# A planner in the source that orders all five engines, longest path first

## The chip, the cores and the metric

One core of one Trainium2 chip. The time is the device time of the whole program in microseconds; lower is better. The core has five engines, each of which works through a list of its own in order: TensorE (PE, with its weight loads PEld), VectorE (DVE), ScalarE (ACT), GpSimd (POOL) and SyncE (SP), which issues all the DMAs. Between engines, an instruction waits for semaphores.

## The reference

One step of a layer with two parallel mixers, for a prompt of 2048 rows and for 8 sequences of 8 new rows ("sample", with a cache of 2048 keys each), all float32:

```python
h = rmsnorm(x, norm_w)
z = h @ w_in                                  # 1024 -> 3600 columns
q, k, v, qb, kb, vb, g_lr, gate_a, gate_b = jnp.split(z, split_points(), axis=-1)
q = rope(rmsnorm(heads(q, H_A), q_norm_w), pos)
k = rope(rmsnorm(heads(k, H_A), k_norm_w), pos)
o_a = attend(q, k, v)                         # three dilated windows, mixed by their softmax sums
log_a = jax.nn.log_sigmoid(g_lr @ w_gate_up + b_gate) / GATE_TAU
o_b, s_fin = gla_chunked(qb, kb, vb, log_a, s0)   # gated linear attention, exact and causal
o_b = rmsnorm(o_b, gla_norm_w)
mixed = jnp.concatenate([o_a * silu(gate_a), o_b * silu(gate_b)], axis=-1)
y = x + mixed @ w_out
```

The three windows are (128, step 1), (512, step 4) and (2048, step 16), with 8 heads of 64. The outputs are y, the rotated keys, the values and the states.

## The kernel before

**Projections.** x is normed in 16 tiles of 128 rows, split into two float16 parts and turned; `project(name, tiles)` multiplies a tile with a block of w_in (v, q, k, qkb, g, vb, gb; 512 columns, g in two halves of 272 and 256) in 24 float16 matmuls into one of two accumulators in PSUM (tag `Y`, names `acc_...`). The results go through VectorE and ScalarE to scratch tensors in device memory (`q_d`, `kp_d`, `vp_d`, ...), and are read back, some by a transposing DMA.

**Attention of the prompt.** `attend` makes a unit of four steps: s (scores, L408), p (a VectorE instruction that masks and finds the maximum, L416, and a ScalarE exponential with its sum, L419), t (transposes on TensorE, L426), pt (the turned p in two float16 parts, by ScalarE and VectorE, or by ScalarE twice and POOL, in turn, L388 to L393) and O (weighted values, L441). Its core:

```python
for n, (q, k) in enumerate(prods):                       # qk, L408
    PE.matmul(s_ps[:, i * w : (i + 1) * w], q, k, ...)
...
DVE.tensor_tensor_reduce(s[:, sl], s_ps[:, sl], mask, neg, BIG, ALU.add, ALU.min, nmf(i))
ACT.activation(s[:, sl], s[:, sl], AF.Exp, bias=nmf(i), scale=-1.0, accum_out=denf(i))
...
PE.transpose(p_ps[:, i * P : (i + 1) * P], t["s"][:, i * P : (i + 1) * P], ident[:])   # tr, L426
split([pt[:, c, w_] for c in range(2)], p_ps[:, w_], t["s"][:, w_])
...
PE.matmul(o_, t["pt"][:, c, ...], vf(i, b), ...)         # pv, L441
```

There are 128 units for the first two windows (two heads each) and 32 for the third (`branch3`, four heads each); `pipeline()` writes them so that three are under way. The tags S, PT and O have two PSUM buffers each.

**The rest.** `sample_scores` multiplies cached keys with queries (POOL `pr`, L980; VectorE `sck`, L981). `gla_core` runs the gated linear attention in seven levels per 256 rows: differences D (POOL), E (ScalarE), ks and qbd (VectorE), sc (TensorE, L247). `prompt_out` gathers a tile's parts (`combine`), turns them (`turned`, tm, L1453) and multiplies by w_out (`finish`, L1488) into two accumulators Y_t_0 and Y_t_1 of 24 matmuls each, which VectorE adds to x (L1495). `sample_pair` does the sample's attention over the cache (OS, L1737); its result goes through the scratch tensor `oa_d` to the sample's own output tile.

**What sets the order.** The Python code is written as generators that `weave` takes steps from in set ratios. The result is the program order, which a scheduler of the framework, with a timeline of its own, turns into one list per engine. Two places bind it: the first tiles' preparation holds ScalarE to the written order, and the loading of the blocks q and k is held behind the last low part of the block before:

```python
with tc.manual_schedule(engines={mybir.EngineType.Activation}):
    prep_first(load_w("v"))
...
with tc.issue_after(last_low[0].ins):
    at_once(load_w("q"))
```

Of the kernel before, what the change touches and what calls it, by code (L numbers as in the profile page):

```python
# [7 lines left out]
F32 = mybir.dt.float32  # L8
F32R = mybir.dt.float32r
F16 = mybir.dt.float16  # L10
BF16 = mybir.dt.bfloat16
# [4 lines left out]
PSUM = bass.MemoryType.PSUM  # L16
DRAM = bass.MemoryType.DRAM

P = 128
# [27 lines left out]
    "vb": (2048, 512),  # L47
    "gb": (3088, 512),
}


@with_exitstack
def tile_hymba(ctx: ExitStack, tc: tile.TileContext, A: dict):
    nc = tc.nc
    PE, ACT, DVE, POOL, SP = nc.tensor, nc.scalar, nc.vector, nc.gpsimd, nc.sync
# [293 lines left out]
    with ExitStack() as c1:  # L349
# [19 lines left out]
        sp = c_att.enter_context(tc.tile_pool(name="sp", bufs=3))  # L369
# [106 lines left out]
        last_low = [None]  # L476
# [189 lines left out]
        def at_once(gen):  # L666
            for _ in gen:
                pass
# [77 lines left out]
        done = set()  # L746
# [271 lines left out]
            return pool.tile([P, 512], F32, name=f"wr_q_{k}", tag=tag)[:]  # L1018

        fetch_w("q", places=q_place)  # L1020
        with tc.manual_schedule(engines={mybir.EngineType.Activation}):
            prep_first(load_w("v"))
        fetch_w("k")

        gnw = const1("gnw", [P, P], A["gla_norm_w"].to_broadcast([P, P]))
# [9 lines left out]
        for nm_, src in (("q", A["q_norm_w"]), ("k", A["k_norm_w"])):  # L1035
            i = "qk".index(nm_)
            w = tabs[:, 0, i]
# [27 lines left out]
        work, side = deque(), deque()  # L1065
# [74 lines left out]
        def first(m):  # L1140
            tiles = list(range(4 * m, 4 * m + 4))
            if m == 0:
                for name in "vqk":
                    for t in (["s"] if name == "v" else []) + tiles:
                        yield from project(name, [t])
                        if name == "v":
                            if t == 0:
                                with tc.issue_after(last_low[0].ins):
                                    at_once(load_w("q"))
                            elif t == 2:  # L1150
                                with tc.issue_after(last_low[0].ins):
                                    at_once(load_w("k"))
                                for f in range(4, 8):
                                    fetch(f)
                        elif name == "k":
                            prep(t + 4)
                            fetch(t + 8)
                return
            for t in tiles:
                for name in "vqk":  # L1160
                    if (name, t) == ("q", 15):
                        at_once(load_w("qkb"))
                    yield from project(name, [t])
                    dot_next(t)
# [27 lines left out]
        order = {"qkb": [12, 13, 14, 15, *range(12)]}  # L1192
# [51 lines left out]
        st = {"wgu": wgu, "E": [], "ks": [], "qbd": []}  # L1244
        for i in range(2):
            for lst, nm_, shape in (
# [3 lines left out]
                t = gst.tile(shape, F32, name=f"{nm_}{i}")  # L1250
# [141 lines left out]
        left = weave(host, gla_all, fetch, until=[host, fetch])  # L1392
# [4 lines left out]
        left = weave(host, gla_all, fetch, until=[gla_all])  # L1397
# [3 lines left out]
        for h in range(4):  # L1401
            p, j = divmod(h, 2)
# [11 lines left out]
        place = lambda t: slice(0, 1) if t == "s" else slice(t + 1, t + 2)  # L1414
# [190 lines left out]
        for nh in range(2):  # L1605
            t = cb1.tile([P, NT + 1], F32, name=f"inv_o{nh}")
# [4 lines left out]
        out = [prompt_out(), 2 * NT * KT + 30]  # L1611
# [180 lines left out]

        weave(out, [sample_attention(), 4 * 16])


# [1 line left out]
_INS = [  # L1797
# [90 lines left out]
```

## Time and profile before

| | |
|---|---|
| median of 3 runs | 1424.39 us (1419.62 to 1426.09) |
| profiled execution, first to last instruction | 1424.9 us; of its own time nothing else is on record, and the span is 0.5 us from the median |
| busy | PE 1285.0, DVE 1018.0, ACT 843.7, POOL 621.9 us |
| mean granted clock of TensorE | 0.966 |
| DMA | 283.27 MB; q1 uses 67.1% of 16 engines' span |

"Busy" of an engine is the time in which at least one of its instructions runs; matmuls overlap each other, so a busy TensorE isn't one at its peak. A line such as `L408 PE MATMUL s<-kk,qq 128*128 128x256 f16 x432 | 93.8, 335 | 17.5 <-DVE o L416 12.4` reads: line 408, engine, operation, output and inputs, shape, how many; busy us in total, mean ns of one; idle us of the engine just before them, and who ended that idle time.

### The profile page before, as it was taken

The numbers are of one execution on the slowest core, as the hardware profiler recorded it, in microseconds if no ns is written. First come the engines' busy times: TensorE is split into PE (matmuls) and PEld (weight loads), VectorE is DVE, ScalarE is ACT, GpSimd is POOL, SyncE is SP. The second block draws the span as 40 slices with busy tenths as digits, with TensorE's granted clock in tenths as the row PEclk, the third lists the DMA queues.
The fourth block names the chain that finished last, engine by engine and source line by source line (L and its number), as shares of the span: only waits on it lengthen the run. The fifth ranks groups of instructions, "written<-read, shape, count | busy, mean of one in ns | idle before, by whom it ended". The sixth has DMA issues, their size and how long they took to land.

```text
span 1424.9 us, 26506 instructions
## 1 busy us (share of the span) xinstructions
PE 1285.0 (90%) x8942; PEld 743.6 (52%) x8942; DVE 1018.0 (71%) x2459; ACT 843.7 (59%) x2259; POOL 621.9 (44%) x564
## 2 busy tenths in 40 slices
PE   5989999889898898996889999889999989999997
PEld 2434555455455554664667666666555434444343
DVE  6797697789798967666775357898877797773222
ACT  6466787667377775875677665777876542221120
POOL 0144355566577455554421486556551264340000
PEclk9999999999999899997999999999999999999998
DMA  8469756678966797888976444242235759998661
GB/s 297 156 188 255 192 161 150 182 203 215 240 165 173 208 288 239 260 217 228 234 190 179 149 123 116 87 153 91 88 119 176 267 179 344 359 316 267 221 215 63
DMA packets 246874, 283.27 MB, mean 199 GB/s; under 512 B 117889, under 2 KB 148690, under 8 KB 246738
## 3 DMA queue, kind: packets, MB, share of 16 engines
q1 hardware_dynamic: 246738, 281.57, 67.1%
q8 instruction: 71, 1.16, 0.4%
q14 instruction: 65, 0.53, 0.1%
HBM read 183.19 MB, written 75.24 MB: 181 GB/s over the span
## 4 chain that ended last, share of the span: by engine, by line
PE 35%; DVE 25%; DMA 16%; ACT 11%; issue 7%; POOL 4%; SPq 2%; DVEq 0%; POOLq 0%; ACTq 0%
PE Y L1488 7%; PE acc_g L1120 3%; PE acc_vb L1120 3%; PE acc_k L1120 3%; DMA k<-in_cache_k_win 2%; POOL pr L980 2%; PE s L408 2%; PE OS L1737 2%; PE acc_qkb L1120 2%; ACT p L419 2%; DMA o_d<-o 2%; DMA oc<-o_d 2%; DVE p L416 2%; PE acc_v L1120 2%; DMA T_q<-qp_d 2%
## 5 line engine op out<-in xcount | busy, mean ns | idle before, releaser
L980 POOL TENSOR_TENSOR pr<-k,qb 128x512 f32<-128x512 f32 x128 | 171.8, 1342 | 184.9 <-DVE sck L981 113.9
L1120 PEld LDWEIGHTS <-hr 128*128 128x128 f16 x1824 | 177.7, 100 | 138.2 <-issue 17.6
L419 ACT ACTIVATE p<-p,o 128x256 f32<-128x256 f32 (+1 forms) x384 | 173.1, 453 | 86.0 <-DVE o L416 83.3
L1120 PEld LDWEIGHTS <-hl 128*128 128x128 f16 x1248 | 123.2, 100 | 146.6 <-issue 22.2
L1488 PE MATMUL Y<-w_o,mh 128*128 128x512 f16 x768 | 182.9, 385 | 8.3 <-ACT mh L1454 4.9
L416 DVE CUSTOM_DVE_ANT_0 p<-s,m3w,scl_s 128x256 f32<-128x256 f32 (+1 forms) x384 | 143.6, 419 | 39.0 <-DMA o_d<-o 20.3
L393 POOL TENSOR_TENSOR pt<-p,pt 128x512 f16<-128x512 f32 (+1 forms) x80 | 98.3, 1229 | 139.6 <-ACT pt L392 107.3
L441 PE MATMUL O<-v,pt 128*128 128x128 f16 x1200 | 116.1, 224 | 25.3 <-POOL pt L393 10.0
L426 PE MATMUL t<-ident,p 128*128 128x128 f32 x600 | 119.0, 289 | 14.5 <-ACT p L419 9.2
L1488 PEld LDWEIGHTS <-mh 128*128 128x128 f16 x768 | 72.5, 99 | 103.7 <-issue 25.2
L408 PE MATMUL s<-kk,qq 128*128 128x256 f16 (+1 forms) x512 | 105.7, 326 | 17.5 <-DVE o L416 12.4
L981 DVE TENSOR_REDUCE sck<-pr 128x8 f32<-128x512 f32 x128 | 87.0, 680 | 44.0 <-POOL pr L980 43.7
L441 PEld LDWEIGHTS <-pt 128*128 128x128 f16 x1200 | 86.6, 101 | 54.6 <-POOL pt L393 13.6
L1120 PE MATMUL acc_g<-w_g,hr 128*128 128x272 f16 (+1 forms) x768 | 103.3, 285 | 1.9 <-DVE so_g L677 1.0
L1120 PE MATMUL acc_v<-w_v,hl 128*128 128x512 f16 x384 | 99.5, 405 | 4.6 <-DMA hl<-ht 3.7
L426 PEld LDWEIGHTS t<-ident,p 128*128 128x128 f32 x600 | 73.5, 146 | 43.2 <-ACT p L419 26.4
L1120 PE MATMUL acc_q<-w_q,hl 128*128 128x512 f16 x384 | 92.0, 380 | 1.9 <-ACT zs_q L703 1.4
L1120 PE MATMUL acc_k<-w_k,hl 128*128 128x512 f16 x384 | 91.3, 382 | 2.5 <-ACT w_k L658 1.3
L1454 ACT ACTIVATE mh<-tm 128x1024 f16<-128x1024 f16 x32 | 31.7, 1019 | 104.1 <-PE tm L1453 97.7
L1120 PE MATMUL acc_gb<-w_gb,hr 128*128 128x512 f16 x384 | 90.0, 388 | 2.1 <-DVE so_gb L677 2.1
L1120 PE MATMUL acc_vb<-w_vb,hr 128*128 128x512 f16 x384 | 89.3, 379 | 1.6 <-DVE so_g L677 1.6
L212 ACT ACTIVATE E<-D_e 128x256 f32<-128x256 f32 (+1 forms) x168 | 67.7, 411 | 27.1 <-DVE ks L219 17.6
(533 smaller groups left out, 2628.1 us busy)
## 6 DMA issues: line engine op xcount, KB each, us to landing
k<-in_cache_k_win SPq DMA_DIRECT2D x104, 256.0 KB, 4.3
sv<-in_cache_v_win SPq DMA_DIRECT2D x104, 256.0 KB, 5.4
hr<-h_d SPq DMA_DIRECT2D x44, 512.0 KB, 4.1
qb<-q_d SPq DMA_DIRECT2D x64, 256.0 KB, 4.6
oc<-o_d SPq DMA_DIRECT2D x48, 264.0 KB, 5.8
o_d<-o SPq DMA_DIRECT2D x64, 132.0 KB, 3.9
x<-in_x_prompt SPq DMA_DIRECT2D x16, 512.0 KB, 5.8
h_d<-hl SPq DMA_DIRECT2D x16, 512.0 KB, 4.7
```

Of the source, the lines that this page charges most:

```text
L212: ACT.activation(E[rows, i, :n], D[rows, half], AF.Exp, scale=1.0 / 16.0)
L393: POOL.tensor_tensor(l, f, h, ALU.subtract)
L408: PE.matmul(s_ps[:, i * w : (i + 1) * w], q, k, start=(n == 0), stop=(n == len(prods) - 1),)
L416: DVE.tensor_tensor_reduce(s[:, sl], s_ps[:, sl], mask, neg, BIG, ALU.add, ALU.min, nmf(i))
L419: ACT.activation(s[:, sl], s[:, sl], AF.Exp, bias=nmf(i), scale=-1.0, accum_out=denf(i))
L426: PE.transpose(p_ps[:, i * P : (i + 1) * P], t["s"][:, i * P : (i + 1) * P], ident[:])
L441: PE.matmul(o_, t["pt"][:, c, (i * nb + b) * P : (i * nb + b + 1) * P], vf(i, b), start=(n == 0), stop=(n == 2 * nb - 1),)
L980: POOL.tensor_tensor(pr[:], kt, qt, ALU.mult)
L981: DVE.tensor_reduce(out, pr[:].rearrange("p (u k d) -> p u k d", u=2, k=4), AX.X, ALU.add)
L1120: PE.matmul(z, a_[:, k, :], w[:, p_, k, cols], start=(k == 0 and i == 0), stop=(k == KT - 1 and i == 2),)
L1454: ACT.activation(mhl[:, a], pt[:], AF.Copy)
L1488: PE.matmul(Y[:], a_[:, k, :], w_[:, part, k, :512], start=(i == 0), stop=(i == len(prods) - 1),)
```

## The change

At the end of the kernel's Python code a class `Plan` reads all the traced instructions, finds what each depends on, gives each a price, and makes a list schedule of its own. Then it chains the instructions of each engine in that order, so that the framework's scheduler has no choice left:

```diff
+class Plan:
+    ENGINES = ("PE", "DVE", "Activation", "Pool", "SP")
+    def __init__(self, tc, nc, cross=35.0, traffic=1.15, lanes=8, room=212832):
...
+        self.read()
+        self.depend()
+        self.price()
...
+                if kind == "InstCustomDveAnt":
+                    late = (211 if by_row else 150) + 1.04 * n
...
+    def rank(self):
...
+            far[n] = max(
+                own + max((far[x] for x in self.nxt[n]), default=0.0),
+                max((far[x] for x in self.then[n]), default=0.0),
+            )
...
+    def order(self, prio, bias=0.0):
...
+            if len(out["SP"]) >= self.lanes:
+                free["SP"] = max(free["SP"], done[out["SP"][-self.lanes]] + self.cross + 20)
...
+            _, n = heappop(line)
+            out[e].append(n)
...
+            if e == "SP":
+                free[e] = t + self.busy[n]
+                queue = max(queue, free[e]) + self.late[n]
+                done[n] = queue + self.lands[n]
...
+                if (n in self.slow) != mode:
+                    s, mode = max(s, max(column) + 93), not mode
...
+    def fix(self, out):
...
+        for e, order in out.items():
+            for a, b in zip(order, order[1:]):
+                self.tc.add_manual_dep(
+                    self.ins[b], self.ins[a].name, info, reason="planned order"
+                )
...
-        with tc.manual_schedule(engines={mybir.EngineType.Activation}):
-            prep_first(load_w("v"))
+        prep_first(load_w("v"))
...
-                                with tc.issue_after(last_low[0].ins):
-                                    at_once(load_w("q"))
+                                at_once(load_w("q"))
...
+    plan = Plan(tc, nc)
+    far = plan.rank()
+    plan.fix(plan.order([-f for f in far], 2000.0)[1])
```

`far[n]` is the length of the longest chain of prices from instruction n to the end of the program. Whenever an engine is free, it takes of its ready instructions the one with the largest `far`. Equal values are taken by turns of the heap, in program order. In the planner a float32 matmul that isn't a transpose (`slow`) costs 93 ns more when the kind changes, and is preferred or put back by 2000 ns so that kinds stay together; a DMA waits until the eighth before it has landed; VectorE and POOL hold each other up where both read two operands from SBUF. Buffers are taken in program order, and a buffer's next tile waits for all users of the last. The number and kind of instructions on every engine stay the same. The two bindings above go. Lines after the class stand 489 further down: L408 is L897, L426 is L915, L1120 is L1608, L1488 is L1974.

Three places of the order. The first is TensorE's list where a unit of the third window (residue 9, first half) passes from s to t; the numbers at the ends of names count tiles. Before, from its last s on:

```order
L408 MATMUL s_3_9_0_8912<-T3_k_9_8879,T3_q_9_8877 128x128
L441 LDWEIGHTS pt_3_7_1_8850
L441 MATMUL O3_7_1_8933<-v3_7_8659,pt_3_7_1_8850 128x128
...
L426 MATMUL t_3_8_0_8901<-ident_79,p_3_8_0_8803 128x128
L441 LDWEIGHTS pt_3_7_1_8850
```

Now:

```order
L897 MATMUL s_3_9_0_8909<-T3_k_9_8876,T3_q_9_8874 128x128
L897 LDWEIGHTS T3_q_9_8874
L897 MATMUL s_3_9_1_8957<-T3_k_9_8876,T3_q_9_8874 128x128
L1608 LDWEIGHTS hr_1_8636
L1608 MATMUL acc_vb_1_10287<-w_vb_8471,hr_1_8636 128x512
L1608 LDWEIGHTS hr_1_8636
L1608 MATMUL acc_g1_1_10254<-w_g_6888,hr_1_8636 128x256
...
L915 MATMUL t_3_9_0_9005<-ident_79,p_3_9_0_8910 128x128
```

The first t of the unit stood 122 rows behind its last s, with steps of units 7 and 8 between them; now it stands 15 rows behind, the two halves of the unit are taken by turns, and projection matmuls of two accumulators fill the place.

The second place is the end of TensorE's list, the last output tile (15). Before:

```order
L1488 MATMUL Y_15_0_16950<-w_o0_13844,mh_15_16842 128x512
L1488 LDWEIGHTS mh_15_16842
L1488 MATMUL Y_15_0_16950<-w_o0_13844,mh_15_16842 128x512
L1488 LDWEIGHTS mh_15_16842
L1488 MATMUL Y_15_1_16976<-w_o1_14251,mh_15_16842 128x512
```

Now:

```order
L1974 MATMUL Y_15_1_16973<-w_o1_14248,mh_15_16839 128x512
L1974 LDWEIGHTS mh_15_16839
L1974 MATMUL Y_15_0_16947<-w_o0_13841,mh_15_16839 128x512
L1974 LDWEIGHTS mh_15_16839
L1974 MATMUL Y_15_1_16973<-w_o1_14248,mh_15_16839 128x512
```

Before, all 24 matmuls of Y_15_0 stood ahead of those of Y_15_1; now the two accumulators take turns to the end, as they do in the other output tiles.

The third place is the end of SP's list: `soo` is the last pair's attention output of the sample, which goes to `oa_d` and comes back as `oa_s`; `xr` are the rows of x to which a tile's output is added. Before:

```order
L1499 DMA out_y_prompt<-xr_14_16804 128x1024
L1781 DMA oa_d_71<-soo_3_16635 64x64 x2
L1477 DMA xr_15_16948<-in_x_prompt 128x1024
L1558 DMA oa_s_16881<-oa_d_71 64x256 x2
L1499 DMA out_y_sample<-xr_s_16907 64x1024
L1499 DMA out_y_prompt<-xr_15_16948 128x1024
```

Now:

```order
L2267 DMA oa_d_71<-soo_3_16632 64x64 x2
L1985 DMA out_y_prompt<-xr_13_16689 128x1024
L2044 DMA oa_s_16878<-oa_d_71 64x256 x2
L1963 DMA xr_s_16904<-in_x_sample 64x1024
L1985 DMA out_y_prompt<-xr_14_16801 128x1024
L1963 DMA xr_15_16945<-in_x_prompt 128x1024
L1985 DMA out_y_sample<-xr_s_16904 64x1024
L1985 DMA out_y_prompt<-xr_15_16945 128x1024
```

The sample's output through `oa_d` stood behind the output of tile 14; now it stands ahead of that of tile 13. On TensorE the last OS matmuls have moved from tile 14 and the transposes of tile 15 to tile 13.

More of the change, by code (lines that the diff above doesn't have):

```diff
@@ L1147, in first @@
                             if t == 0:
-                                with tc.issue_after(last_low[0].ins):
-                                    at_once(load_w("q"))
+                                at_once(load_w("q"))
                             elif t == 2:
-                                with tc.issue_after(last_low[0].ins):
-                                    at_once(load_w("k"))
+                                at_once(load_w("k"))
                                 for f in range(4, 8):
```

423 lines of the change are left out of this document (added).

## The prediction

> **What bounds the kernel now.** I read the page first, then the clock, the busy times by stage, the groups by form, and single stretches of the timeline.
>
> ```profile
> span 1424.9 us, 26506 instructions
> ...
> PE 1285.0 (90%) x8942; PEld 743.6 (52%) x8942; DVE 1018.0 (71%) x2459; ACT 843.7 (59%) x2259; POOL 621.9 (44%) x564
> ...
> core 0: 1424.9 us, clock 0.966
> ...
> PE 35%; DVE 25%; DMA 16%; ACT 11%; issue 7%; POOL 4%; SPq 2%; DVEq 0%; POOLq 0%; ACTq 0%
> ```
>
> TensorE is the engine to keep fed: it is busy 1285.0 of 1424.9 us, so 139.9 us are plain idle. The granted clock of 0.966 costs up to 1424.9 x 0.034 = 48 us more. But only 35% of the chain that ended last is TensorE; VectorE, ScalarE, DMAs and issue hold most of the rest. That is the picture of an order that leaves TensorE waiting, here for one engine and there for another. The next view says where; its columns are the stage, its length, then busy us of PE, PEld, DVE, ACT and POOL with instruction counts, the clock, the DMA share and GB/s.
>
> ```profile
> 0.00:100.00 100.00, 77.49 (x385) 36.57 (x385) 76.82 (x177) 56.37 (x104) 19.44 (x29) 1.00 0.63 211
> 100.00:400.00 300.00, 274.74 (x1732) 157.17 (x1733) 244.27 (x572) 201.44 (x570) 158.91 (x122) 0.97 0.76 200
> 400.00:500.00 100.00, 87.02 (x592) 54.98 (x591) 89.59 (x205) 74.53 (x207) 62.90 (x48) 0.93 0.69 187
> 500.00:600.00 100.00, 92.93 (x633) 56.58 (x631) 67.86 (x181) 71.37 (x202) 57.47 (x46) 0.97 0.90 260
> 600.00:700.00 100.00, 81.94 (x608) 55.12 (x607) 69.63 (x216) 65.07 (x206) 47.95 (x39) 0.88 0.86 231
> 700.00:800.00 100.00, 95.11 (x841) 69.98 (x839) 62.72 (x259) 78.14 (x283) 22.92 (x22) 1.00 0.69 176
> 800.00:900.00 100.00, 98.34 (x743) 61.93 (x741) 59.99 (x122) 57.18 (x149) 69.38 (x82) 1.00 0.44 124
> 900.00:1000.00 100.00, 87.39 (x812) 62.91 (x813) 87.06 (x184) 79.21 (x211) 58.31 (x70) 0.97 0.37 118
> 1000.00:1100.00 100.00, 91.18 (x722) 54.53 (x719) 81.11 (x170) 74.28 (x184) 43.62 (x51) 0.98 0.41 130
> 1100.00:1200.00 100.00, 88.89 (x493) 42.80 (x491) 79.37 (x177) 45.68 (x89) 40.72 (x34) 0.95 0.74 251
> 1200.00:1400.00 200.00, 192.90 (x1333) 83.72 (x1326) 93.96 (x200) 40.08 (x61) 40.25 (x31) 0.99 0.79 268
> 1400.00:1425.00 25.00, 17.07 (x68) 7.29 (x68) 5.66 (x8) 0.38 (x1) 0.00 (x0) 0.82 0.13 43
> ```
>
> Length minus PE busy gives the idle: 22.5 us in the first stage (start-up), 68.3 in 100 to 800 (projections woven with attention), 23.1 in 800 to 1100 (gated linear attention), 26.1 in 1100 to 1425 (output projection woven with the sample attention). Stages of the same kind differ: 18.1 us are lost in 600:700 and 4.9 in 700:800; 12.6 in 900:1000 and 1.7 in 800:900. The clock is low exactly where the idle is: 0.88, 0.93, 0.95, 0.82. One wait of each kind:
>
> ```profile
> 657.57 0.47 PE L426 MATMUL t<-ident,p 128*128 128x128 f32 x1 [5.30 <-ACT p L419]
> ...
> 1402.51 0.69 PE L1465 MATMUL mt_s<-ident,mix_s 64*128 64x64 f32 x4 [4.11 <-DVE mix_s L1566]
> ```
>
> After the 5.30 us wait stands the stage with clock 0.88. [...] So idle costs twice, and I let the clock loss follow the idle.
>
> **The change, term by term.** No instruction is added or taken away on any engine's data path; the terms are waits that go and waits that come. I sum against the profiled span, 1424.9 us; the median of the runs is 1424.39, so nothing is corrected between them.
>
> *Attention, 100 to 800.* The chain of one unit is s (matmul), p (VectorE, ScalarE), t (transposes), pt (two halves), O (matmul). Its steps:
>
> ```profile
> L419 ACT ACTIVATE p<-p,o 128x256 f32<-128x256 f32 x216 | 107.8, 501 | 60.2 <-DVE o L416 57.5 <-issue 1.9
> L416 DVE CUSTOM_DVE_ANT_0 p<-s,m3w,scl_s 128x256 f32<-128x256 f32 x216 | 95.1, 476 | 26.0 <-DMA o_d<-o 9.1 <-POOL pr L980 6.8 <-POOL pt L393 4.4
> L393 POOL TENSOR_TENSOR pt<-p,pt 128x512 f16<-128x512 f32 x70 | 87.9, 1256 | 109.9 <-ACT pt L392 85.7 <-DVE o L416 15.9 <-DVE qp L815 3.6
> ...
> L419 ACT ACTIVATION_READ_ACCUMULATOR p<-p,o 128x1 f32 x384 | 72.8, 190 | 0.0
> ...
> L389 DVE SCALAR_TENSOR_TENSOR pt<-t,pt 128x512 f16<-128x512 f32 x70 | 47.8, 683 | 11.4 <-ACT pt L388 11.0
> ...
> L392 ACT ACTIVATE pt<-p 128x512 f16<-128x512 f32 x70 | 43.6, 623 | 0.6
> L391 ACT ACTIVATE p<-t 128x512 f32<-128x512 f32 x70 | 41.0, 586 | 3.6 <-PE t L426 3.2
> L388 ACT ACTIVATE pt<-t 128x512 f16<-128x512 f32 x70 | 40.8, 583 | 13.2 <-PE t L426 13.2
> ...
> L416 DVE DVE_READ_ACCUMULATOR2_ANT o<- 128x1 f32 x384 | 30.9, 81 | 0.0
> ```
>
> From the last s to the first t pass at least 2 x (0.476 + 0.081) + 0.501 + 0.190 = 1.81 us; from t to O 0.583 + 0.683 = 1.27 us by the short way or 0.586 + 0.623 + 1.256 = 2.47 by the long one. I counted in both orders how much TensorE work (matmul columns at their back-to-back pitch) stands between. Before, s to t has a median of 6.3 us over the 160 units, t to O 5.0 over 128. Now it is 3.4 and 3.9. Where less work stands there than the chain lasts, TensorE must wait: summed, that was 0 us (s to t) and 1.2 to 8.5 (t to O, all units short way to all long), and is now 5.7 and 8.0 to 51.1; at half and half, 35 us. So the new order can't be idle for much less than 40 us in this part, where now it is 68.3: -28 us. The bounds: 14 us idle (the short way everywhere) gives -54; a gain of nothing is the slower rival's ground.
>
> *Gated linear attention, 800 to 1100.* Levels of the chain D, E, ks, qbd, sc depend on each other; the planner may put projection matmuls in between. I let the two bad stages (12.6 and 8.8) come to the 4.9 of 700:800: -12 us; bounds 0 and -21.
>
> *Output, 1100 to 1425.* The 11.1 us of 1100:1200 come to the 3.6 per 100 us of 1200:1400: -7.6. At the end the sample's attention now closes one tile earlier, and 48 matmuls of tile 14 cover the way of its result through memory; the 4.11 us wait quoted above goes: together -12; bounds 0 and -20.
>
> *New: accumulators that end together.* The order switches the accumulator 2332 times between neighbouring projection or output matmuls, 206 times before; Y_t_0 and Y_t_1 now end side by side, so both evacuations lie between a tile and the next.
>
> ```profile
> L1495 DVE SCALAR_TENSOR_TENSOR xr<-Y,inv_o,xr 128x512 f32<-128x512 f32 x32 | 23.7, 744 | 68.8 <-PE Y L1488 59.5 <-DMA xr<-in_x_prompt 9.1
> ...
> 1410.00 10.52 PE L1488 MATMUL Y<-w_o,mh 128*128 128x512 f16 x48
> ...
> 1389.33 2.75 PE L1488 MATMUL Y<-w_o,mh 128*128 128x512 f16 x12
> 1392.02 0.62 PE L1737 MATMUL OS<-sv,P3x 128*32 128x256 f32 x2
> ```
>
> Back to back a Y matmul takes 10.52 / 48 = 0.22 us, so before, the 24 of Y_t_1 (5.2 us) hid the 0.744 of Y_t_0. Now two evacuations, 1.49 us, are hidden only by what the order puts there, transposes tm and some OS matmuls. I take 0.5 us on 15 tiles, +7; bounds 0 and 15 x 1.49 = +22. Changes between full-width and narrow matmuls (64 or 32 columns) cost: the twelfth Y starts near 1389.33 + 11 x 0.216 = 1391.70, OS at 1392.02, 0.10 more than the pitch. There were 298 of them, now 326: +3.
>
> *Queues.* On SP every DMA stays, in another order: writes and loads still wait in line behind one that isn't ready. Neither SP nor POOL (44% busy) holds the chain by more than 4%, so I price this at 0; without that cover it is in the slower rival.
>
> *Start.* The first 100 us keep their 22.5 us: the same weights come through the same queue before the first full tile. Bounds -10 and +5.
>
> *Clock.* Idle falls from 140 to 140 - 28 - 12 - 12 = 88 us; the 48 us in proportion to 30: -18. Bounds -35 and 0.
>
> Sum: 1424.9 - 28 - 12 - 12 + 7 + 3 - 18 = 1365 us. With its terms' bounds this case reaches from 1315 to 1410.
>
> **Rivals.** *Slower: just in time is too late.* The same shorter distances leave no reserve. Engines run their lists in order, so a late p or pt stops TensorE though other ready matmuls stand behind it. That such lateness exists, these rows show:
>
> ```profile
> L727 POOL TENSOR_TENSOR t_qk<-zs_q,ct_qk 128x1024 f32<-128x1024 f32 x12 | 28.4, 2363 | 8.0 <-issue 4.4 <-ACT zs_q L703 3.6
> L125 DVE TENSOR_SCALAR rv_qk<-qs_q 128x16 f32<-128x16 f32 x12 | 20.4, 1699 | 0.2
> L125 DVE TENSOR_SCALAR rv_o_c<-oss_c 128x4 f32<-128x4 f32 x16 | 4.5, 283 | 0.0
> ```
>
> The same line takes 0.28 us in one place and 1.70 in another, with a long POOL operation (2.36 us) near. The old 6.3 us took such a 1.4 us delay in; in the new order half of the units have 1.6 us or less above the 1.81. Price: 160 + 128 waits; at 0.2 us each (58) the gain is gone, at 0.28 (81) the time is 1446. For it: DVE is 90% busy in 400:500. Against: a late wait delays, but later ones overlap with it, and the planner's prices of VectorE and ScalarE lie near these rows (its 477 ns for the 476).
>
> *Fuller gain.* If the order hid all but the start and some 15 us, idle would be 38: 1424.9 - 102 - 35 + 3 = 1291. Against it stands the 35 us count above.
>
> *VectorE is the bound.* Busy 244 of 300 and 90 of 100 us with its waits inside, it leaves the attention and the linear attention as they are; only the 12 of the output with 4 of clock go, against +10: 1419. Against: 63 to 68 busy in 500:600 and 700:800, where idle is still 5 to 7.
>
> *Alternating accumulators throttle.* If switching accumulators halved the clock, the 768 Y matmuls would cost 0.216 us more each, +166: 1531. The trace has such a stretch, acc_v and acc_v_s in turn:
>
> ```profile
> 27.00 0.81 PE L1120 MATMUL acc_v<-w_v,hl 128*128 128x512 f16 x3
> 27.64 0.59 PE L824 MATMUL acc_v_s<-w_v,hs 128*128 128x512 f16 x2
> ```
>
> Three matmuls in 0.64 us is the full pitch, in a stage with clock 1.00. [...]
>
> **How the numbers follow.** Forecast 0.52; just in time too late 0.24; fuller gain 0.13; VectorE bound 0.08; throttling 0.03. A difference under 0.5% (7 us) can't be told from none here. Faster: 0.52 + 0.13 + 0.01 of the VectorE case = 0.66. Same: 0.07, the rest of that case. Slower: 0.24 + 0.03 = 0.27. The range goes from 1285 to 1450: outside are some 0.05 of the fuller gain, 0.10 of the slower rival and the throttling. The likeliest case alone: 1315 to 1410.
>
> **What would show it.** Right: PE idle near 90 us, about 40 of it in the attention, no wait of 4 us at the end, clock about 0.978. Slower rival: t waiting for ACT p and O for pt often and for 0.2 to 0.5 us, attention's idle at or above 68. Wrong altogether: a DMA or SP's queue at the top of the waits, a start much longer than now, or a Y pitch above 0.22 us.

## The result and the profile after

The changed kernel takes 1408.38 us (median of 4 runs, 1403.16 to 1409.20), the kernel before beside it 1425.24 (4 runs, 1419.62 to 1427.01). The ratio is 0.9876, with a 95% interval of 0.9850 to 0.9902: 1.2% faster, where 4.2% was forecast. The sign was right and the time lies inside the range; more than half of the gain is missing. The profiled execution took 1407.61 us. Its page, the lines of span, engines and the chain that ended last:

```profile
span 1405.7 us, 26555 instructions
...
PE 1280.0 (91%) x8942; PEld 745.2 (53%) x8942; DVE 1012.9 (72%) x2459; ACT 844.8 (60%) x2259; POOL 640.1 (46%) x564
...
PE 35%; DMA 10%; DVE 6%; ACT 6%; issue 3%; POOL 2%; SPq 1%; DVEq 0%; ACTq 0%; POOLq 0%
```

TensorE's idle is 1405.7 - 1280.0 = 125.7 us (139.9 before, 88 forecast). The granted clock of 0.971 costs up to 41 us (48 before, 30 forecast). The busy times by stage, cut as in the prediction (length, then busy us of PE, PEld, DVE, ACT and POOL, clock, DMA share, GB/s):

```profile
0.00:100.00 100.00, 82.09 (x406) 38.89 (x407) 80.21 (x187) 60.38 (x113) 22.59 (x31) 1.00 0.71 227
...
500.00:600.00 100.00, 98.03 (x725) 63.83 (x723) 75.86 (x212) 79.48 (x228) 54.31 (x43) 1.00 0.83 242
600.00:700.00 100.00, 89.22 (x706) 58.06 (x704) 67.56 (x253) 73.94 (x258) 32.02 (x26) 0.98 0.93 228
...
1000.00:1100.00 100.00, 87.32 (x664) 51.38 (x662) 85.79 (x162) 72.74 (x181) 62.00 (x61) 0.91 0.37 119
1100.00:1200.00 100.00, 77.73 (x522) 36.32 (x520) 66.78 (x175) 34.89 (x74) 33.27 (x28) 0.86 0.79 260
1200.00:1400.00 200.00, 196.79 (x1308) 93.56 (x1306) 105.29 (x204) 44.27 (x64) 44.55 (x33) 1.00 0.75 255
```

The start, the attention and the output proper (1200 to 1400) are better than before, 1000 to 1200 is worse: 34.95 us idle in these 200 us at clocks of 0.91 and 0.86, where before it was 19.9 us at 0.98 and 0.95. Three wider stretches show it, in the kernel before first, then in the changed one (PE busy, clock, DMA share, GB/s):

```profile
100.00:800.00 700.00, 631.74 (x4398) 0.95 0.77 208
800.00:950.00 150.00, 140.98 (x1128) 0.98 0.44 128
950.00:1150.00 200.00, 178.07 (x1350) 0.97 0.45 147
```

```profile
100.00:800.00 700.00, 642.28 (x4543) 0.98 0.81 212
800.00:950.00 150.00, 145.14 (x1178) 0.98 0.36 105
950.00:1150.00 200.00, 163.97 (x1158) 0.88 0.45 146
```

From 100 to 800 the idle falls from 68.3 to 57.7 us and the clock loss from 700 x 0.05 = 35 to 14. From 950 to 1150 the idle grows from 21.9 to 36.0 us and the clock loss from 6 to 24. These clock losses are upper bounds, since a low clock costs nothing while TensorE stands idle anyway: from 1129 to 1143 us it reads 0.50 with no matmul running. Cut into slices of 1 us and counted by the busy part of each slice, the clock costs 26 us before and 10 now in 100 to 800, and 4 before and 13 now in 950 to 1150. With the idle, some 26 us are won in the attention and 23 lost behind it. So most of what the attention brought is gone before the output begins: the first `tm`, the transposes ahead of an output tile, starts at 1142.3 us before and at 1146.2 now. The start, 800 to 950 and the output make the rest. The transposes that open the linear attention say when it starts. Of `ptg_smp` (the sample's) and `ptg_e` (the prompt's, eight steps of 256 rows in a chain) the view of one tile gives count, least, median and longest ns, first and last start; before, then after:

```profile
L166 PE MATMUL ptg_smp<-ident,zqk_smp x4: 222/222/272, 808.8 to 809.0; 64*128 64x64 f32 x4
L166 PE MATMUL ptg_e<-ident,zqk_e x64: 272/273/377, 816.4 to 1012.5; 128*128 128x128 f32 x64
```

```profile
L655 PE MATMUL ptg_smp<-ident,zqk_smp x4: 222/271/273, 775.1 to 776.2; 64*128 64x64 f32 x4
L655 PE MATMUL ptg_e<-ident,zqk_e x64: 272/273/330, 813.0 to 1048.9; 128*128 128x128 f32 x64
```

The sample's part starts 34 us earlier, the prompt's 3 us earlier, and the transposes of its last step come 36 us later than before. In between, the new order has put the g and vb projections and the sample's states. The waits of the changed kernel that the text uses (us in total, times, longest) and the timeline at the seam between linear attention and output:

```profile
PE ts_q L2123 <- DMA ls_q<-q_d: 18.4, 1, 18.4
...
PE s L897 <- DVE o L905: 17.5, 20, 2.4
...
DVE p L905 <- DMA o_d<-o: 14.3, 10, 3.4
...
PE acc_gb L1608 <- DVE so_gb L1166: 7.8, 3, 4.2
...
PE t L915 <- ACT p L908: 5.0, 8, 1.5
...
PE t L915 <- DVE pt L878: 4.0, 4, 2.1
...
PE O L930 <- POOL pt L882: 3.0, 3, 1.8
...
PE O L930 <- DVE pt L878: 2.4, 5, 0.9
```

```profile
1120.64 2.75 PE L1608 MATMUL acc_gb<-w_gb,hr 128*128 128x512 f16 x12
1123.23 0.27 PE L1066 MATMUL mx_o<-ident,w_o 128*1 128x128 f32 x1
...
1143.24 0.69 PE L2123 MATMUL ts_q<-ident,ls_q 64*128 64x64 f32 x4 [18.37 <-DMA ls_q<-q_d]
```

The gb projection, the last work that depends on nothing new, ends at 1123. Soon after, TensorE stands for 18.37 us, by the label for a load of the sample's q.

### The profile page after: what moved, and what is told of

It reads as the page before. It is cut to its first block, busy times and chain, and to the rows that moved or that the text cites. A ratio compares the mean times of both kernels' runs of the same rounds, so it can differ in the third digit from the quotient of the medians.

```text
span 1405.7 us, 26555 instructions
## 1 busy us (share of the span) xinstructions
PE 1280.0 (91%) x8942; PEld 745.2 (53%) x8942; DVE 1012.9 (72%) x2459; ACT 844.8 (60%) x2259; POOL 640.1 (46%) x564
## 4 chain that ended last, share of the span: by engine, by line
PE 35%; DMA 10%; DVE 6%; ACT 6%; issue 3%; POOL 2%; SPq 1%; DVEq 0%; ACTq 0%; POOLq 0%
PE Y L1974 9%; PE acc_vb L1608 4%; PE acc_gb L1608 4%; PE acc_g L1608 3%; DMA oc<-o_d 2%; PE OS L2223 2%; DMA k<-in_cache_k_win 2%; DMA ga_d<-so_g 2%; PE acc_qkb L1608 1%; POOL pr L1469 1%; ACT p L908 1%; PE sc_e L736 1%; PE s L897 1%; DMA sv<-in_cache_v_win 1%; PE t L915 1%
## 5 line engine op out<-in xcount | busy, mean ns | idle before, releaser
L1608 PEld LDWEIGHTS <-hr 128*128 128x128 f16 x1824 | 175.0, 99 | 124.5 <-issue 28.7
L1608 PEld LDWEIGHTS <-hl 128*128 128x128 f16 x1248 | 121.8, 100 | 130.5 <-issue 17.8
L1974 PE MATMUL Y<-w_o,mh 128*128 128x512 f16 x768 | 183.0, 381 | 1.5 <-DVE xr_s L1981 0.8
L905 DVE CUSTOM_DVE_ANT_0 p<-s,m3w,scl_s 128x256 f32<-128x256 f32 (+1 forms) x384 | 142.1, 420 | 29.2 <-DMA o_d<-o 14.3
L882 POOL TENSOR_TENSOR pt<-p,pt 128x512 f16<-128x512 f32 (+1 forms) x80 | 90.7, 1134 | 143.5 <-ACT pt L881 104.7
L930 PE MATMUL O<-v,pt 128*128 128x128 f16 x1200 | 140.5, 223 | 6.6 <-POOL pt L882 3.0
L915 PE MATMUL t<-ident,p 128*128 128x128 f32 x600 | 131.3, 289 | 9.7 <-ACT p L908 5.0
L1608 PE MATMUL acc_g<-w_g,hr 128*128 128x272 f16 (+1 forms) x768 | 130.6, 276 | 3.3 <-ACT vbs L1266 2.0
L897 PE MATMUL s<-kk,qq 128*128 128x256 f16 (+1 forms) x512 | 112.2, 323 | 19.9 <-DVE o L905 17.5
L1608 PE MATMUL acc_vb<-w_vb,hr 128*128 128x512 f16 x384 | 120.9, 379 | 4.7 <-DVE so_g L1166 4.7
L930 PEld LDWEIGHTS <-pt 128*128 128x128 f16 x1200 | 98.4, 101 | 47.4 <-issue 9.2
L1608 PE MATMUL acc_q<-w_q,hl 128*128 128x512 f16 x384 | 117.8, 383 | 5.4 <-ACT zs_q L1192 5.3
L1470 DVE TENSOR_REDUCE sck<-pr 128x8 f32<-128x512 f32 x128 | 87.2, 681 | 47.3 <-POOL pr L1469 46.6
L1608 PE MATMUL acc_v<-w_v,hl 128*128 128x512 f16 x384 | 119.3, 387 | 1.7 <-ACT zs_k L1192 0.9
L1608 PE MATMUL acc_k<-w_k,hl 128*128 128x512 f16 x384 | 115.5, 379 | 4.3 <-DVE vp L1279 1.7
L1974 PEld LDWEIGHTS <-mh 128*128 128x128 f16 x768 | 71.1, 98 | 87.6 <-issue 14.0
L915 PEld LDWEIGHTS t<-ident,p 128*128 128x128 f32 x600 | 78.9, 145 | 50.5 <-ACT p L908 25.5
L1608 PE MATMUL acc_gb<-w_gb,hr 128*128 128x512 f16 x384 | 95.6, 399 | 7.8 <-DVE so_gb L1166 7.8
L1608 PE MATMUL acc_qkb<-w_qkb,hr 128*128 128x512 f16 x288 | 86.0, 379 | 0.0
```

Source lines behind the costliest of these rows:

```text
L882: POOL.tensor_tensor(l, f, h, ALU.subtract)
L897: PE.matmul(s_ps[:, i * w : (i + 1) * w], q, k, start=(n == 0), stop=(n == len(prods) - 1),)
L930: PE.matmul(o_, t["pt"][:, c, (i * nb + b) * P : (i * nb + b + 1) * P], vf(i, b), start=(n == 0), stop=(n == 2 * nb - 1),)
L1470: DVE.tensor_reduce(out, pr[:].rearrange("p (u k d) -> p u k d", u=2, k=4), AX.X, ALU.add)
L1608: PE.matmul(z, a_[:, k, :], w[:, p_, k, cols], start=(k == 0 and i == 0), stop=(k == KT - 1 and i == 2),)
L1974: PE.matmul(Y[:], a_[:, k, :], w_[:, part, k, :512], start=(i == 0), stop=(i == len(prods) - 1),)
```

## The experiments

Four theories stood at the outset. A: the planner spends the independent projection matmuls early, so that the serial chain of the linear attention and the seam stand bare. B: the attention's shorter distances make TensorE wait for late steps. C: accumulators that alternate cost time. D: the load `ls_q` comes too late. Each kernel below is the changed kernel with an edit of its last three lines or of the planner's numbers (`wr[n]` is the tile that instruction n writes); beside each median of 4 runs stands the ratio to the kernel before on the same chip, with its 95% interval. The changed kernel's is 0.9876.

**filler_last.**

```
 prio = [-f for f in far]
+for n in real:
+    if wr[n].startswith(("acc_g", "acc_vb", "acc_qkb")):
+        prio[n] += 50000.0
```

> The matmuls of the projections g, vb, gb and qkb get the lowest priority in the planner (50 us less than their path), so that they stand only where nothing else is ready. Theory A (filler spent early): the changed kernel's 42 us of earlier attention are lost from 950 to 1150 us, where TensorE was idle for 36 us and lost 23 us to the clock, because the projections that could fill the linear attention's waits were done before it. Then the prompt's first ptg, at 813 us, comes some 40 to 50 us earlier, idle and clock loss of 950 to 1150 halve, and the time falls by 25 to 35 us to 1375 to 1385. Theory B (just in time too late): the attention's waits hold the time, which this doesn't touch: within 7 us of 1408. Theory C (accumulators that end together) and theory D (the late load ls_q): within 7 us as well, with the wait of 18 us for ls_q still there under D.

1380.25 us, 0.9700 (0.9665 to 0.9735). The same three stretches, and the first transposes of the prompt:

```profile
100.00:800.00 700.00, 642.24 (x4526) 0.98 0.81 212
800.00:950.00 150.00, 144.39 (x1286) 1.00 0.38 118
950.00:1150.00 200.00, 186.69 (x1281) 0.97 0.54 181
```

```profile
L655 PE MATMUL ptg_e<-ident,zqk_e x64: 270/273/330, 759.6 to 1008.5; 128*128 128x128 f32 x64
```

The attention is as it was (57.8 us idle). From 950 to 1150 the idle is 13.3 us instead of 36.0 and the clock 0.97 instead of 0.88, and the prompt's chain starts 53 us earlier. The time lies in theory A's range.

**seam_after_y0.**

```
+end = max(n for n in real if wr[n].startswith("Y_0_0_"))
+for n in real:
+    if plan.eng[n] == "PE" and wr[n].startswith(("ts_q", "ts_k", "R_0_")):
+        plan.behind[n].add(end)
...
```

> The transposes ts_q, ts_k and the first R may only stand behind the last matmul of Y_0_0; priorities as in the changed kernel. Theory D (the late load): the 18.4 us wait for ls_q and the half clock behind it (some 11 us) go, time 1380 to 1390. Theory A: the wait was only put down to the load; the chain of the first mix (oc loads at 1121, mix at 1136 to 1137, mt, tm) would have held TensorE until about 1139 in any case, so that 3 to 7 us are won: 1401 to 1405. Theories B and C: no change by more than 5 us.

1413.83 us, 0.9927 (0.9900 to 0.9955): not faster than the changed kernel. Its timeline at the seam:

```profile
1124.83 0.38 PE L1069 MATMUL mx_o<-mm_o,one_row 1*128 1x1 f32 x2 [0.99 <-DVE mm_o L1068]
1145.28 1.04 PE L1939 MATMUL tm<-ident,mt 128*128 128x128 f16 x8 [20.07 <-ACT mt L1929]
```

With `ts_q` out of the way TensorE waits 20.07 us for `mt`, the parts of the first mixed tile. The loads for that tile go out late too; SP's queue in the changed kernel:

```profile
1121.02 0.32 SPq L1263 DMA_DIRECT2D gw_d<-gw  x1
1121.39 1.40 SPq L1991 DMA_DIRECT2D oc<-o_d  x3
```

From there to its first `tm`, at 1146, pass 25 us. Theory D falls, and even the 3 to 7 us that theory A allowed were not there: the load `ls_q` was the last of several things that came late, and the label names the last. The loads of oc read the attention's output, whose last store went out at 763. In SP's list they stand right behind the store of `gw`, which GpSimd made from a late gb projection from 1119.7 to 1121.0 us; all of this is on the chain that ended last. So here the place of the loads in SP's list counts. Whether an earlier place alone would help was not tried.

**plan_first_part, plan_second_part.** The planner's order is kept for one half of the program only; the scheduler of the kernel before orders the other half.

```
+cut = min(n for n in real if wr[n].startswith("zqk_smp"))
+plan.fix({e: [n for n in o if n < cut] for e, o in out.items()})    # or n >= cut
```

> Only the instructions written before the sample's linear attention (start, q, k, v and qkb projections, attention) keep the planner's order; all behind stands as the scheduler of the kernel before puts it. Theory A (what attention wins is lost where the plan orders the rest): the attention ends near 756 us as in the changed kernel, the rest keeps the filler that it had before, and the time is 1395 to 1405, at or below the changed kernel's 1408. Theory E (the rest of the plan is no worse, the gain of the attention is just not there): 1415 to 1425.

> Only the instructions from the sample's linear attention on (g, vb and gb projections, linear attention, output, sample attention) keep the planner's order; all ahead of them stands as the scheduler puts it. Theory A: 950 to 1150 us loses some 30 us to idle and clock against the kernel before, as in the changed kernel, the output stage wins some 19 to 22: 1420 to 1435. Theory E: the plan's output stage is a gain that comes through, 1400 to 1410.

The first half alone takes 1395.05 us, 0.9786 (0.9763 to 0.9810), less than both halves together. The second half alone takes 1460.54 us, 1.0245 (1.0219 to 1.0271), 36 us slower than the kernel before. First-half kernel, then second-half kernel:

```profile
L655 PE MATMUL ptg_smp<-ident,zqk_smp x4: 221/223/274, 782.9 to 783.2; 64*128 64x64 f32 x4
L655 PE MATMUL ptg_e<-ident,zqk_e x64: 272/273/474, 788.4 to 997.1; 128*128 128x128 f32 x64
```

```profile
L655 PE MATMUL ptg_smp<-ident,zqk_smp x4: 222/272/272, 828.4 to 829.5; 64*128 64x64 f32 x4
L655 PE MATMUL ptg_e<-ident,zqk_e x64: 272/273/473, 866.2 to 1099.8; 128*128 128x128 f32 x64
```

Where the scheduler orders the rest, the prompt follows 5.5 us after the sample; where the planner does, 37.8 us (37.9 in the changed kernel, 7.6 before, 9.2 in filler_last). The first `ptg_smp` and the first `tm` cut each profiled span in three. The table has the length of each part and, in brackets, TensorE's idle in it, in us:

| kernel | up to the first ptg_smp | from there to the first tm | from there to the end |
|---|---|---|---|
| before | 808.8 (90.8) | 333.5 (26.1) | 282.6 (23.0) |
| changed | 775.1 (75.4) | 371.1 (40.4) | 259.5 (9.9) |
| plan_first_part | 782.9 (71.9) | 332.0 (33.2) | 279.6 (20.5) |
| plan_second_part | 828.4 (114.2) | 369.2 (38.8) | 258.6 (9.0) |
| filler_last | 750.4 (74.8) | 359.3 (16.0) | 266.9 (12.2) |

Where the planner orders the second half, the linear attention is some 37 us longer and the output 21 to 23 us shorter, whichever order the first half has. Not all of that is waiting, as work also changes its part: between kernel before and changed kernel the idle alone differs by 14 us more and 13 less. So the loss sits in the linear attention as the planner orders it, and the planner's output is a gain. The second half alone is slower than theory A's 1420 to 1435 because the part ahead of it got worse too: it is 20 us longer than before although the scheduler orders it, with 23 us more idle. Why was not tried.

**gla_path_longer.**

```
+for n in gla:    # instructions that touch a tile of the linear attention
+    plan.late[n], plan.busy[n] = plan.late[n] * 1.5, plan.busy[n] * 1.5
 far = plan.rank()    # and back to their own values for the order
```

> No lower priority for any projection; the linear attention's instructions only count 1.5 times in the length of the path that ranks them, so that their chain goes ahead. Theory A in the form that the late start of the serial chain is the loss: the prompt's first ptg comes some 50 us earlier (760 to 770 instead of 813), the stretch before the output is better filled, 1380 to 1393. If what counts is only which matmuls are left at its end (the gb projections), and these end no later than now, 1400 to 1410.

1395.59 us, 0.9807 (0.9782 to 0.9832). The prompt's chain starts at 750 us, even earlier than in filler_last, and 950 to 1150 is idle for 18.7 us at a clock of 0.96; yet 15 us less is won than there. From the first `ptg_smp` to the first `tm` TensorE is idle for 17.4 us, about as in filler_last (16.0). So ranking the chain ahead of the projections fills this part as ranking the projections behind the chain does. Where the other 15 us go isn't shown; the runs with random priorities below differ by as much.

**attention_slack, store_price.**

```
+for n in real:    # attention_slack
+    if plan.eng[n] != "PE" and wr[n].startswith(("p_1_", "p_2_", "p_3_", "pt_1_", "pt_2_", "pt_3_")):
+        plan.late[n] += 300.0
```

```
+for n in real:    # store_price: the 80 stores of a tile o
+    if plan.eng[n] == "SP" and any(not w and t.startswith(("o_1_", "o_2_", "o3_")) ... for t, w, _ in plan.acc[n]):
+        plan.lands[n] += 1500.0
```

> Each softmax and split step (writes of p and pt on VectorE, ScalarE and GpSimd) is priced 0.3 us later in the planner, so that its order leaves 0.6 us more between s and t and 0.3 to 0.9 us more between t and O. Theory B (just in time too late): the idle of 100 to 800 us falls from 57.7 to some 35, with clock, and the time to 1380 to 1390. Theory A: the idle in the attention changes by less than 10 us, and what is won there is lost again before 1150: 1400 to 1412. Theories C and D: no change.

1393.04 us, 0.9786 (0.9766 to 0.9807): 15 us less, but not where theory B said. The idle of 100 to 800 us is 56.1 us, as before the edit. The longest sum of waits in the attention is that of s, and one row of VectorE and the TensorE row that follows, from the timeline of the changed kernel, show what stands behind it:

```profile
206.09 0.35 DVE L905 CUSTOM_DVE_ANT_0 p<-s,m3w,scl_s 128x128 f32<-128x128 f32 x1 [3.12 <-DMA o_d<-o]
```

```profile
206.77 1.01 PE L897 MATMUL s<-kk,qq 128*128 128x256 f16 x4 [1.88 <-DVE o L905]
```

p writes its minimum and sum into a tile o whose last content is still on its way to memory; s gets no accumulator until p has read the old one. In attention_slack itself p waits longer for these stores, 25.4 us, and s less, 13.9. The next run prices these stores later.

> The changed kernel, with the landing of the 80 stores of the attention's tile o (o_d) priced 1.5 us later in the planner; it has them at 2.4 us plus their turn, and the profile shows 4.0 us from issue to landing. In the changed kernel s waits 17.5 us for VectorE's step p, and that step waits 14.3 us for these stores, since its minimum and sum go into a tile o that is still being stored. Theory S (these stores set the attention's idle): both waits fall by half or more, idle in 100 to 800 from 57.7 to about 45, time 1393 to 1400. If the four tiles o are simply too few, the planner can't place around it and the waits stay: 1403 to 1412.

1392.01 us, 0.9770 (0.9737 to 0.9802). Both waits shrink, from 17.5 us (s) and 14.3 us (p), and the idle of 100 to 800 falls to 49.3:

```profile
PE s L897 <- DVE o L905: 10.7, 9, 3.7
...
DVE p L905 <- DMA o_d<-o: 1.5, 2, 0.8
```

The wait for the stores is nearly gone, but more than half of the wait of s is left, where theory S had both halved. So by this run the stores stand behind some 7 of the 17.5 us; behind the rest is VectorE for other reasons, which no run takes apart.

**jitter_1, jitter_2, jitter_3.** Both gains above are of a size that a plan might reach by chance, so three runs changed no price.

```
+rng = random.Random(1)    # 2, 3
-plan.fix(plan.order([-f for f in far], 2000.0)[1])
+plan.fix(plan.order([rng.uniform(-300.0, 300.0) - f for f in far], 2000.0)[1])
```

> The changed kernel with a random number between -0.3 and +0.3 us added to every instruction's priority; no price is changed. If the attention's order is decided by such small differences (plans of equal merit differ by chance), this moves the time by 10 us or more either way, and the -15 of attention_slack and the -16 of store_price can't be put down to their prices alone. If the prices are the cause: 1402 to 1414.

> As jitter_1 with other random numbers: by chance, between 1388 and 1425, apart from jitter_1 by 8 us or more; if the prices are the cause: 1402 to 1414.

> As jitter_1 with a third set: by chance, between 1388 and 1425; if the prices are the cause: 1402 to 1414.

1401.87, 1394.12 and 1398.68 us (0.9836, 0.9783, 0.9801, each within 0.0043). A reshuffle alone moves the time by up to 14 us, and the changed kernel was the slowest of the four. So the times of attention_slack and store_price are not shown to come from their prices, and the same holds for the 13 us of gla_path_longer and of plan_first_part; what store_price does show is the wait that it removes. The 28 us of filler_last are twice a reshuffle. And the hole after 950 us stands in all three, with 34 to 38 us of idle against 13.3 in filler_last:

```profile
950.00:1150.00 200.00, 162.25 (x1166) 0.91 0.45 149
```

```profile
950.00:1150.00 200.00, 165.07 (x1213) 0.90 0.48 156
```

```profile
950.00:1150.00 200.00, 165.97 (x1188) 0.91 0.47 151
```

**one_accumulator.**

```
+for n in real:    # all matmuls of an accumulator take the priority of its first
+    if plan.eng[n] == "PE" and wr[n].startswith(("acc_", "Y_")):
+        first[wr[n]] = min(first.get(wr[n], 0.0), prio[n])
...
```

> All matmuls of one accumulator (acc of the projections, Y of the output) get the priority of its first, so that neighbouring accumulators no longer alternate: 242 switches instead of 2332. Theory C (accumulators that end together cost 0.5 us on 15 tiles, up to 1.49): the time falls by 7 us, at most by 22: 1386 to 1401. Theory A: Y tiles gain nothing since their stage was at clock 1.00 with 3 us idle in 200; the time stays within 6 us of 1408. Theories B and D: no change.

1405.31 us, 0.9886 (0.9857 to 0.9916): no difference from the changed kernel. For the output's Y, theory C falls. For the projections it stays open. There too two accumulators end together, and TensorE's waits before the prompt's acc matmuls sum to 14.5 us before, 26.8 in the changed kernel and 13.4 here (14.8 to 24.2 in the three random orders). What is saved there comes back in other waits: those of O go from 7.1 to 15.8 us, those of sc_e, in the linear attention, from 4.5 to 10.2.

**sp_unplanned.** `del out["SP"]` ahead of `plan.fix(out)`.

> The planner's order for TensorE, VectorE, ScalarE and GpSimd only; SP's DMAs stand as the scheduler puts them. The prediction priced SP's order at 0: within 7 us of 1408. If the planned places of the loads are part of the gain, 1415 or more; if SP's order is part of the loss (loads in line behind writes that aren't ready, as at the first mix), 1400 or less.

1441.74 us, 1.0124 (1.0105 to 1.0143): 33 us slower than with SP planned, and slower than the kernel before. From 100 to 800 it is idle for 73.6 us instead of 57.7, and the first `tm` comes at 1168 instead of 1146. The planned places of the loads belong to the planned order of the engines; as the run sets one scheduler's loads against another's order, it doesn't say what SP's new order is worth against the old.

**Towards a better version.** filler_last_slack puts the edits of filler_last and attention_slack together. acc_last gives all projections, q, k and v too, the lowest priority, with 0.15 us more on p and pt; acc_last_grouped adds the edit of one_accumulator; the last two add 0.3 instead of 0.15 us, and store_price's edit.

> filler_last and attention_slack together: lowest priority for the projections g, vb, gb and qkb, and 0.3 us more in the price of each softmax and split step. If both work in different places (A at 950 to 1150, B in the attention, as their runs say, -28 and -15 us), they add up to 1362 to 1370. If the slack run's gain came through the same hole, what is left is 1376 to 1384.

> acc_last_grouped (1346 us) without the common priority of an accumulator's matmuls: projections last, 0.15 us more on each softmax and split step, accumulators alternate again. If the grouping brings nothing, as one_accumulator said (-3 us), 1343 to 1353; if accumulators that end together cost what the prediction priced (+7, up to 22), 1353 to 1368.

> All projections get the lowest priority (q, k and v too), all matmuls of one accumulator the same one, and each softmax and split step 0.15 us more. Theory A with B: projections as filler everywhere, so the attention's idle of 57 us falls as well, by some 15; 1345 to 1365. If the waits in the attention are for s accumulators that VectorE has not yet read (17.5 us of them in the changed kernel), as a rival says, filler there brings nothing more: 1365 to 1380.

> acc_last_grouped with 0.3 instead of 0.15 us added to the price of each softmax and split step. Theory B (lateness in the attention still costs): some 5 us less than 1346, 1338 to 1344. If with filler everywhere the attention no longer waits for late steps, 1344 to 1354.

> acc_last_grouped (1346 us) with the same later landing of the stores of o. Theory S: its 18.9 us of s waiting for VectorE's step p halve, time 1333 to 1340. If the tiles o are too few whatever the order: 1343 to 1352.

| kernel | us | ratio to before |
|---|---|---|
| filler_last_slack | 1370.20 | 0.9607 (0.9578 to 0.9635) |
| acc_last | 1364.42 | 0.9583 (0.9558 to 0.9608) |
| acc_last_grouped | 1346.19 | 0.9445 (0.9419 to 0.9472) |
| acc_last_grouped_300 | 1352.28 | 0.9492 (0.9460 to 0.9524) |
| grouped_store_price | 1356.04 | 0.9523 (0.9497 to 0.9549) |

acc_last_grouped beats both kernels, by 5.5% and 4.4%; its page:

```profile
PE 1257.9 (94%) x8942; PEld 733.7 (55%) x8942; DVE 1008.4 (75%) x2459; ACT 843.3 (63%) x2259; POOL 637.2 (47%) x564
```

Of its span of 1344.4 us 86.5 are idle, 46.6 of them between 100 and 800, and its clock is 0.986. The steps among these five (grouping -18, slack +6, stores +10) are of the size of a reshuffle, and the -18 stand against the -3 of one_accumulator: alone they name no cause. Two of the runs say more. acc_last, with alternating accumulators, came out in theory C's range. With late projections the waits before the acc matmuls are 13.0 to 15.2 us in the three runs that alternate (acc_last, filler_last, filler_last_slack) and 1.6 to 5.2 in the three grouped ones, and every grouped run is faster than every alternating one. So grouping may well be worth something there. grouped_store_price lies outside both of its ranges: p hardly waits for stores any more (0.4 us), s waits 12.3 us instead of 18.9, and still the time is 10 us longer, against theory S. That late projections carry the gain is common to all five, and to filler_last: the six runs with them take 1346 to 1380 us, all the others 1392 and more.

## Why the prediction was wrong, and where it was right, by its own steps

**Linear attention (-12): the failed step.** I let bad stages come to the level of good ones and did not ask which work the planner would put into the gaps. Idle went from 23.1 to 19.8 us in 800 to 1100, and from the first `ptg_smp` to the first `tm` it rose from 26.1 to 40.4, with 8 us more of clock. Longest path first ranks a projection by the chain behind it, not by its worth as filler: the chain of eight steps waited 38 us behind it at the start and had nothing beside it at the end. filler_last, gla_path_longer and plan_first_part show this, each from its side.

**Output (-12): right, once the seam is over.** In the prediction's own cut, from 1100 on, idle went from 26.1 to 30.3 us. But that takes in the seam, with its single wait of 18.37 us. From the first `tm` on it fell from 23.0 to 9.9.

**Attention (-28, to 40 us idle): mis-sized, -10.6.** The count of matmul work between s, t and O gave 35 us of waits. Measured between 100 and 800 us, t and O waited for p and pt 14.4 us (t 5.0 and 4.0, O 3.0 and 2.4), against 33 before: fewer, not more. What the step left out are the other waits. s waits for VectorE to free its accumulator, 17.5 us now and 12.7 before; projections wait for theirs; and p waits for the store of o, 14.3 us now and 20.3 before. The row that the prediction quotes for p had the last: "26.0 <-DMA o_d<-o 9.1". I read that row for its duration only. The clock of this stage gave some 16 us, nearly the whole 18 that I counted for all stages.

**The end: right.** The sample's last transposes and sums no longer wait 4 us; the view of the timeline has:

```profile
1380.52 0.46 PE L1951 MATMUL mt_s<-ident,mix_s 64*128 64x64 f32 x4
1380.91 0.62 PE L1939 MATMUL tm<-ident,mt 128*128 128x128 f16 x8
1382.49 7.08 PE L1974 MATMUL Y_s<-w_o,mh_s 128*128 128x512 f16 x32 [0.97 <-DVE mh_s L1957]
1390.34 10.59 PE L1974 MATMUL Y<-w_o,mh 128*128 128x512 f16 x48 [0.76 <-DVE xr_s L1981]
```

**Accumulators that end together (+7): not where I put it.** All Y matmuls of the kernel have 1.5 us of idle before them, against 8.3 before, and one_accumulator came out at 1405 against 1408 us.

```profile
L1974 PE MATMUL Y<-w_o,mh 128*128 128x512 f16 x768 | 183.0, 381 | 1.5 <-DVE xr_s L1981 0.8
```

The waits that grew stand before the projections, where two accumulators end together too: 26.8 us against 14.5. I priced none there. The last 48 matmuls of Y run at 10.59 / 48 = 0.22 us each, and 1200 to 1400 stands at clock 1.00 with alternating accumulators, so the throttling rival is out as well: no run shows that switching halves the clock, and what the changed kernel shows in its place is the 0.22 us of before (10.52 / 48).

**Type changes (+3)** were not measured apart. **Queues (0): open.** "Neither holds the chain" said nothing of what SP's order is worth. At the seam the loads of oc stand behind a store that isn't ready, and sp_unplanned is 33 us slower, but no run prices the new order of SP alone. **Start (0):** -4.6 us, within its bounds.

**Clock (-18): -7, or -10 (39 to 29 us) counted by the busy slices.** It falls with idle, as forecast, but the proportion was my estimate, and the changed kernel doesn't show it: 100 to 800 loses 10 us to the clock at 57.7 us of idle, 950 to 1150 loses 13 at 36.0. In slices of 5 us the clock falls during the 18.37 us wait to 0.50 and comes back only around 1155, 12 us after the matmuls do. Behind the longest wait of acc_gb, 4.2 us until 1021.5, it reads 0.50 from 1020 to 1025. It also goes to 0.50 behind a wait of 2.2 us (at 981) and one of 3.2 us with shorter ones ahead of it (at 1091), while behind one of 2.1 us (at 375) it stays at 1.00: the length of a wait alone doesn't say whether the clock falls. And "exactly where the idle is" doesn't hold for the first stage: it had 22.5 us of idle at 1.00. Yet matmuls start 0.43 us apart there until about 26 us and 0.21 after, with 1.00 recorded on both sides, so the recorded clock of the first 26 us can't be taken at its word.

**The range.** The prediction's own sign of being wrong altogether, a DMA at the top of the waits, came true for TensorE: its longest wait is labelled with the load `ls_q`. The time still lies in the range, at the edge of the likeliest case's 1315 to 1410. How these two follow from the terms isn't said: their lower bounds add up to 1288.

**The rivals.** "Just in time is too late" named the right place and the wrong wait: t and O got better. "VectorE is the bound" comes nearest in the attention, where s waits for VectorE. VectorE itself waited for a store in part of these waits.

## What to carry to other kernels

A list scheduler that takes the longest path first can spend independent work early; give work that only has to be done sometime a lower rank than the serial chain, and look at how bare the chain stands at its end. Follow a wait back through the engine that it names: s waited for VectorE, VectorE in part for a store, and a load named at a seam was only the last to come. Cut the time at events (a first transpose, a first output matmul) as well as at fixed times, or a wait that moves changes its stage. Before a gain of 1% between two orders is put down to a price, reshuffle the order with no price changed: here that alone moved 14 us.

## What was not expected of the hardware

Between 950 and 1150 us the changed kernel's clock was 0.88 although TensorE was busy for 164 of 200 us; with the projections spread over the same stretch (filler_last) it was 0.97 at 187 us. So with 23 us less idle the upper bound of the clock loss is 200 x 0.03 = 6 us instead of 24. The attention's stores of tile o took 4.0 us from issue to landing in the median (the page's list of DMA issues: KB each, us), and a store can hold TensorE through VectorE, as at 206 us, where p waits 3.12 us for it and s 1.88 us for VectorE:

```profile
o_d<-o SPq DMA_DIRECT2D x64, 132.0 KB, 4.0
```

The last 48 matmuls of Y take 10.59 us in the changed kernel, where the accumulators alternate, and 10.52 before, where they don't. If the 46 more switches make the difference, that is 1.5 ns for each; over the 2126 more switches of the whole order, an estimate from these two figures is 3 us.
